# Two-bank product tiles in the first block, paired score matmuls, and groups 4,4,4,4,2,4 in one feed-forward stage

## The chip, the cores and the metric

The kernel runs on one core of one Trainium2 chip. The metric is the device time of one execution in microseconds (us). Three executions of the kernel before took 3538.49, 3545.83 and 3560.31 us; the median is 3545.83 us. The engines are named as the profile names them: PE (TensorE, matrix products; its weight loads are PEld), DVE (VectorE), ACT (ScalarE), POOL (GpSimd), SP (SyncE, which issues the DMAs). PSUM, the memory that PE writes its products to, has eight banks; one bank holds 512 float32 for each of the 128 partitions.

## The reference, cut to what matters

Two blocks follow each other on a sequence of 512 tokens of width 1024, all in float32. What the change touches is in the first block (two layers) and in the first feed-forward stage of the second block.

```python
# first block, for each of 2 layers
h = rms_norm(x, attn_norm[l]); proj = h @ w_in[l]
ret_o = retention(...)                  # 6 heads, chunks of 128
nsa_o = nsa(...)                        # 6 heads, 2 key/value groups; keys and values also compressed to 31 blocks
gm_o  = spatial_gating(...)
x = x + concat(ret_o, nsa_o, gm_o) @ w_out[l]
h = rms_norm(x, ffn_norm[l])
gate, up = split(h @ w_gate_up[l])      # 2 x 2816 columns
x = x + (silu(gate) * up) @ w_down[l]
# inside nsa, for a selected and a window branch
s = q @ k.T + bias; p = masked_softmax(s); o = p @ v
# second block, layer 0 (deltanet), its feed-forward, on 512 latent and 256 context columns
x = layernorm(alpha * x + g * ((silu(h @ w_gate) * (h @ w_up)) @ w_down))
# then layer 1: differential attention "da" and another feed-forward
```

## The kernel before, in words

Every float32 product of activations and weights is made of three matmuls (`mm3`, L216 to L220): both operands are split in a rounded part `hi` and a rest `lo`, and hi·hi, hi·lo and lo·hi are added in PSUM. A weight tile is loaded by a DMA on SP's queue (`wraw`, L205), `whi` is copied by ACT (L212), and `wlo` is made by DVE (L213).

Activations are held transposed, [128 features, tokens]. `gemm_b` makes a [128, 512] product in one PSUM bank (tile `gb`); `gemm_a` makes four token tiles t0 to t3 in four banks (tiles `ga0` to `ga3`) and calls an evacuation for each as soon as the last matmul of that tile is written down. In the first block's phase, `ps("g", ...)` gives one of four single banks (`g=4`, L856); the other four banks are s (2), o and c.

The program is written stage by stage, and a scheduler places each engine's instructions by priorities, taking its own estimates of when inputs are ready; afterwards each engine runs its list strictly in order. An instruction that must wait holds up all that stands behind it on its engine. Waits are semaphore counts of another engine's list. A wait is added wherever an instruction touches a tile that an instruction ahead of it in program order on another engine reads or writes, and tiles are what the tracking knows: two halves of one tile count as the same tile in the built program.

Places that the prediction speaks of:

- Feed-forward of the first block (`ffn1`): three groups of 8, 8 and 6 chunks. A chunk makes a gate product `pg` and an up product `pu` (24 matmuls each), and DVE and ACT turn them into an activation: `g` (L825), tanh (ACT, L826), `u` (L827), L828, L829, `ahi` (ACT, L830), `alo` (L831). After a group, eight down products, one for each m, are added to `x` by DVE (L836). Between them DVE also carries the filler `ada` (L901), a long product of its own.
- `gemm_a`: 14 of them in the two layers. The evacuations read the bank by ACT (L404, L410, L503, L695, L735), and by ACT and DVE for keys and values (`vt`, L493).
- Compression in `nsa`: for j = 0 and 1, a `gemm_b`, then `c` (DVE, L534), `X` (DVE, L538), and 64 small matmuls `pc` (L543) with `w1`, which a DMA brings (L531). In layer 0, DVE copies of bias tables (`biasc`) that come by DMA stand ahead of `c`.
- Scores in `nsa` (L614 to L625): for a pair of heads g = 0, 1 and a tile t, a matmul `S` (L619) on half of the partitions each, and DVE's bias and maximum (L622).
- The feed-forward `ffn2(0)` of the second block: the groups are FOURS (L31). After the last group, the down products of the context columns (256) and of the latent columns (512) are made for m = 0 to 7; DVE adds each to `xa` (L1459) and to two sums `lacc` (L1328, L1329); the layer norm's matmul `lns` (L1340) needs the finished sums. On PE `lns` of the latent columns stands ahead of the projections `da` of the next stage.

Of the kernel before, what the change touches and what calls it, by code (L numbers as in the profile page):

```python
# [14 lines left out]
F32 = mybir.dt.float32  # L15
# [7 lines left out]
P = 128  # L23
# [4 lines left out]
DFF = 2816  # L28
NFF = 22
GROUPS = ((0, 8), (8, 8), (16, 6))  # L30
FOURS = ((0, 4), (4, 4), (8, 4), (12, 4), (16, 4), (20, 2))  # L31
NEG = -1e30
NCMP = 31
NCTX = 256
# [155 lines left out]
class Kern:  # L190
# [29 lines left out]
        nc.tensor.matmul(out, l[1], r[0], start=False, stop=stop)  # L220

    def ps(self, tag, name):
        return self.psum.tile([P, 512], F32, name=name, tag=tag, bufs=self.banks[tag])

    def phase(self, **banks):

        self.banks = banks
        return self.tc.tile_pool(name="psum", bufs=1, space=PSUM, reuse_waits="tile")

    def gemm_a(self, h, dram, n, evac, tiles=NT):  # L230
# [221 lines left out]
    def nsa(self, l, mp, h, rt, rr, mix, early):  # L452
        tc, nc, a = self.tc, self.nc, self.a
        with tc.tile_pool(name=f"nsa{l}", bufs=1, reuse_waits="tile") as np_:
            kT = np_.tile([P, 2, T], F32, name="kT")
            vt = np_.tile([P, NT, 256], F32, name="vt")
            qT = np_.tile([P, 3, T], F32, name="qT")
# [6 lines left out]
            for g in range(2):  # L464
                s = slice(64 * g, 64 * g + 64)
# [7 lines left out]
            with tc.tile_pool(name=f"nsp{l}", bufs=1, reuse_waits="tile") as nw:  # L473
# [35 lines left out]
                for b in range(2):  # L509
                    ps = self.ps("s", "kps")  # L510
# [3 lines left out]
                for p in range(3):  # L514
                    ps = self.ps("s", "qps")
# [10 lines left out]
            with tc.tile_pool(name=f"cmp{l}", bufs=1, reuse_waits="tile") as cp, tc.tile_pool(name=f"nsw{l}", bufs=1, reuse_waits="tile") as nw:  # L526
                pc = self.ps("c", "pc")
                for j in range(2):
# [3 lines left out]
                    ps, = self.gemm_b(lambda k: (h[0][:, k], h[1][:, k]), KD, a["w_cmp"][l, j], ((0, T),))  # L532
                    c = cp.tile([P, T], F32, name="c", bufs=CB["c"])
# [6 lines left out]
                    for li in range(32):  # L540
                        for g in range(2):
                            s = slice(64 * g, 64 * g + 64)
# [10 lines left out]
                for g in range(2):  # L553
                    s = slice(64 * g, 64 * g + 64)
# [53 lines left out]
                for p in range(3):  # L608
                    po = self.ps("o", "po")
                    heads = (p, p + 3)  # L610
                    for b in range(2):
                        Z = nw.tile([P, 2, NT], F32, name="Z", bufs=2)
                        Pt = [[nw.tile([P, (t + 1) * P], F32, name=f"P{g}{t}", bufs=2) for t in range(NT)] for g in range(2)]
                        for t in range(NT):  # L614
                            n = (t + 1) * P
                            for g in range(2):
                                s = slice(64 * g, 64 * g + 64)
                                ps = self.ps("g", "S")
                                nc.tensor.matmul(ps[:, :n], qT[s, p, t * P:(t + 1) * P], kT[s, b, :n], start=True, stop=True)  # L619
                                sb = nw.tile([P, T], F32, name="sb", bufs=3)  # L620
                                mx = nw.tile([P, 1], F32, name="mx", bufs=4)
                                nc.vector.tensor_tensor_reduce(sb[:, :n], ps[:, :n], self.bias[:, heads[g], (3 - t) * P:],  # L622
                                                               -1.0, 3e38, op0=OP.add, op1=OP.min, accum_out=mx)
                                nc.scalar.activation(Pt[g][t], sb[:, :n], AF.Exp, bias=mx[:, 0:1], scale=-1.0,
                                                     accum_out=Z[:, g, t:t + 1])  # L625
                        early(3 + 2 * p + b, cp)
                        r = nw.tile([P, 2, NT], F32, name="r", bufs=2)
                        nc.vector.reciprocal(r, Z)
                        for g in range(2):
                            nc.vector.tensor_tensor(r[:, g], r[:, g], gate[:, :, heads[g] * 3 + 1 + b], op=OP.mult)  # L630
                        for t in range(NT):
                            for g in range(2):
                                nc.vector.tensor_scalar(Pt[g][t], Pt[g][t], r[:, g, t:t + 1], None, op0=OP.mult)
                        for j in range(NT):
                            n = (NT - j) * P
                            pts = []
                            for g in range(2):
                                ps = self.ps("s", "PT")
                                for t in range(j, NT):
                                    self.tpose(ps[:, (t - j) * P:(t - j + 1) * P], Pt[g][t][:, j * P:(j + 1) * P])  # L640
                                pt = nw.tile([P, T], F32, name="pt", bufs=3)
                                self.copy(pt[:, :n], ps[:, :n])
                                pts.append(pt)
                            for g in range(2):
                                nc.tensor.matmul(po[64 * g:64 * g + 64, j * P:], vt[:, j, b * P + 64 * g:b * P + 64 * g + 64],
                                                 pts[g][:, :n], start=b == 0 and j == 0, stop=False)
                    for g in range(2):
                        ps = self.ps("c", "PcT")
                        for t in range(NT):
                            self.tpose(ps[:NCMP, t * P:(t + 1) * P], scs[p][:, g, t])  # L650
                        pt = nw.tile([NCMP, T], F32, name="pct", bufs=2)
                        self.copy(pt, ps[:NCMP])
                        nc.tensor.matmul(po[64 * g:64 * g + 64], vc[:, 64 * g:64 * g + 64], pt, start=False, stop=True)
                    nc.scalar.activation(mix[0][:, p], po, AF.Copy)
                    nc.vector.tensor_tensor(mix[1][:, p], po, mix[0][:, p], op=OP.subtract)
# [188 lines left out]
    def first_block(self, depth=2):  # L844
        tc, nc = self.tc, self.nc
        self.xd = self.dram.tile([P, KD, T], F32, name="xd")
        self.xsrc = self.a["xT"]
        with tc.tile_pool(name="stat1", bufs=1, reuse_waits="tile") as self.stat, tc.tile_pool(name="mixc", bufs=1, reuse_waits="tile") as self.mixc:
            self.attn_norm = self.const("attn_norm", self.mixc)
            self.x_open()  # L850
            self.ffn_norm = self.const("ffn_norm", self.mixc)
            for nm in ("rope_c", "rope_s", "decay", "zeta", "xi", "cdec", "upper"):
                setattr(self, nm, self.const(nm, self.mixc))
            self.filler = self.ada()
            self.turns = TURNS[0]
            with self.phase(g=4, s=2, o=1, c=1) as self.psum:  # L856
                self.bias = self.mixc.tile([P, 6, T], F32, name="bias")
                self.biasc = self.mixc.tile([P, 6, NT, NCMP], F32, name="biasc")
                for l in range(depth):
                    self.layer1(l)  # L860
                    self.ffn1(l, l == depth - 1)
                    self.xsrc = self.xd
                for _ in self.filler:
                    pass
                self.filler = iter(())
            self.x_close()
# [996 lines left out]
```

## Time and profile before

| What | Value |
| --- | --- |
| Median of three runs | 3545.83 us (3538.49 to 3560.31) |
| Profiled execution | 3552.48 us, span 3550.7 us |
| Mean granted PE clock | 0.965 |
| PE busy | 3369.4 us, 95% of the span |
| PEld busy | 2814.8 us, 79% |
| DVE busy | 2343.1 us, 66% |
| ACT busy | 1504.6 us, 42% |
| POOL busy | 169.8 us, 5% |

All times in the rows further down are microseconds from the start of the span. In a timeline row the columns are: start, duration, engine, line, operation, output tile<-input tiles, shape, number of instructions, and in brackets the idle time of the engine just before it with what ended it. Matmuls overlap, so the distance from one start to the next is what a matmul costs, not its duration. The granted clock is a fraction of full speed: 1.00 is 2.4 GHz and 0.50 is 1.2 GHz.

### The profile page before, as it was taken

What the parts mean: (1) busy time and instruction counts of PE and PEld (TensorE: products, weight loads), DVE (VectorE), ACT (ScalarE), POOL (GpSimd) and SP (SyncE); (2) the same over time, 40 slices, a digit from 0 to 9 for tenths busy, and PEclk for the clock granted to TensorE, in tenths of its full rate; (3) what the DMA queues carried; (4) which work ended last, traced back from release to release, by engine and by line L of the source; (5) the groups of instructions that cost most, each with busy time, mean ns of one, the idle gap of its engine ahead of it and who ended that gap; (6) DMA issues with size and microseconds to landing.
All of it is one profiled execution on the core that took longest, in us unless ns stands there. A gap on an engine that the chain in (4) does not pass through costs nothing.

```text
span 3550.7 us, 54927 instructions
## 1 busy us (share of the span) xinstructions
PE 3369.4 (95%) x21774; PEld 2814.8 (79%) x21774; DVE 2343.1 (66%) x4749; ACT 1504.6 (42%) x2818; POOL 169.8 (5%) x161
## 2 busy tenths in 40 slices
PE   8999999989999999998999899999996999989998
PEld 6767888877678888777888777999996877778887
DVE  4556996545569854587778779676667566674336
ACT  4442322334433222456667657333336444452224
POOL 1000000010000000000010000111100000000000
PEclk9999999999999999999999899999998999999999
DMA  5212674331136843321111123222213211233333
GB/s 188 58 46 93 194 223 130 105 104 45 45 98 193 258 136 105 117 60 39 39 53 42 62 84 107 71 72 69 69 55 107 81 42 42 60 113 116 96 96 112
DMA packets 123306, 339.34 MB, mean 96 GB/s; under 512 B 17249, under 2 KB 35953, under 8 KB 122536
## 3 DMA queue, kind: packets, MB, share of 16 engines
q1 hardware_dynamic: 123048, 335.82, 30.9%
q8 instruction: 171, 2.80, 0.3%
q14 instruction: 87, 0.71, 0.1%
HBM read 324.16 MB, written 14.75 MB: 95 GB/s over the span
## 4 chain that ended last, share of the span: by engine, by line
PE 76%; DVE 11%; ACT 5%; issue 3%; DMA 3%; POOL 2%; SPq 0%; POOLq 0%; DVEq 0%; ACTq 0%
PE gb L218 14%; PE gb L219 14%; PE gb L220 14%; PE w L220 2%; PE w L218 2%; PE w L219 2%; DVE wlo L213 2%; DMA wada<-ada_w 2%; PE S L1595 2%; PE ga L220 2%; PE ga L218 2%; PE ga L219 2%; PE S L619 1%; PE da L220 1%; ACT whi L212 1%
## 5 line engine op out<-in xcount | busy, mean ns | idle before, releaser
L212 ACT ACTIVATE whi<-wraw 128x1024 fp32r<-128x1024 f32 (+4 forms) x519 | 472.5, 912 | 1081.7 <-PE gb L219 717.7
L213 DVE TENSOR_TENSOR wlo<-wraw,whi 128x1024 fp32r<-128x1024 f32 (+4 forms) x519 | 538.9, 1039 | 275.8 <-ACT whi L212 270.0
L220 PE MATMUL gb<-fhhi,wlo 128*128 128x512 f32 x704 | 276.1, 392 | 3.5 <-DVE wlo L213 3.4
L218 PE MATMUL gb<-fhhi,whi 128*128 128x512 f32 x704 | 275.7, 392 | 3.2 <-ACT fhhi L325 3.2
L219 PE MATMUL gb<-fhlo,whi 128*128 128x512 f32 x704 | 275.6, 392 | 0.0
L901 DVE CUSTOM_DVE_ANT_0 ada_t<-wada,ada_s 128x1024 f32<-128x1024 f32 x160 | 195.4, 1221 | 22.7 <-DMA wada<-ada_w 21.5
L218 PE MATMUL gb<-dhhi,whi 128*128 128x256 f32 (+1 forms) x528 | 193.8, 371 | 8.2 <-ACT dhhi L917 7.1
L218 PE MATMUL gb<-bhi,whi 128*128 128x512 f32 (+1 forms) x576 | 196.6, 343 | 2.6 <-ACT bhi L1816 1.8
L219 PE MATMUL gb<-blo,whi 128*128 128x256 f32 (+1 forms) x576 | 196.4, 342 | 0.1
L220 PE MATMUL gb<-bhi,wlo 128*128 128x512 f32 (+1 forms) x576 | 196.3, 342 | 0.1
L219 PE MATMUL gb<-dhlo,whi 128*128 128x256 f32 (+1 forms) x528 | 192.0, 365 | 0.1
L220 PE MATMUL gb<-dhhi,wlo 128*128 128x256 f32 (+1 forms) x528 | 190.5, 362 | 0.0
L218 PE MATMUL ga<-whi,hhi 128*128 128x384 f32 (+2 forms) x448 | 164.2, 366 | 14.8 <-ACT hhi L325 11.0
L219 PE MATMUL ga<-wlo,hhi 128*128 128x384 f32 (+2 forms) x448 | 163.3, 364 | 3.3 <-DVE wlo L213 3.3
L220 PE MATMUL ga<-whi,hlo 128*128 128x384 f32 (+2 forms) x448 | 163.2, 365 | 0.0
L220 PEld LDWEIGHTS gb<-fhhi,wlo 128*128 128x128 f32 x704 | 133.1, 189 | 33.9 <-DVE wlo L213 6.3
L1459 DVE SCALAR_TENSOR_TENSOR xa<-gb,mod,xa 128x256 f32<-128x256 f32 (+1 forms) x128 | 77.9, 615 | 123.0 <-PE gb L220 122.1
L218 PEld LDWEIGHTS gb<-fhhi,whi 128*128 128x128 f32 x704 | 133.0, 189 | 31.3 <-ACT fhhi L325 4.0
L219 PEld LDWEIGHTS gb<-fhlo,whi 128*128 128x128 f32 x704 | 133.2, 189 | 27.7
L219 PE MATMUL da<-wlo,ahhi 128*128 128x256 f32 x512 | 147.8, 289 | 1.0 <-DVE wlo L213 1.0
L218 PE MATMUL da<-whi,ahhi 128*128 128x256 f32 x512 | 148.0, 289 | 0.0
L220 PE MATMUL da<-whi,ahlo 128*128 128x256 f32 x512 | 147.1, 287 | 0.0
(569 smaller groups left out, 8749.8 us busy)
## 6 DMA issues: line engine op xcount, KB each, us to landing
wada<-ada_w SPq DMA_DIRECT2D x96, 512.0 KB, 4.4
wraw<-f_gate SPq DMA_DIRECT2D x52, 512.0 KB, 3.6
wraw<-f_up SPq DMA_DIRECT2D x52, 512.0 KB, 3.6
wraw<-w_gate SPq DMA_DIRECT2D x44, 512.0 KB, 4.2
wraw<-w_up SPq DMA_DIRECT2D x44, 512.0 KB, 4.0
wraw<-da_in SPq DMA_DIRECT2D x40, 512.0 KB, 3.6
wraw<-w_down SPq DMA_DIRECT2D x32, 512.0 KB, 3.8
wraw<-dn_in SPq DMA_DIRECT2D x32, 512.0 KB, 3.7
```

The source lines that it names most:

```text
L212: self.nc.scalar.activation(hi[:, :n], raw, AF.Copy)
L213: self.nc.vector.tensor_tensor(lo[:, :n], raw, hi[:, :n], op=OP.subtract)
L218: nc.tensor.matmul(out, l[0], r[0], start=start, stop=False)
L219: nc.tensor.matmul(out, l[0], r[1], start=False, stop=False)
L220: nc.tensor.matmul(out, l[1], r[0], start=False, stop=stop)
L619: nc.tensor.matmul(ps[:, :n], qT[s, p, t * P:(t + 1) * P], kT[s, b, :n], start=True, stop=True)
L901: nc.vector.tensor_tensor_reduce(th, w, s[:, st], 0.5, 0.0, op0=OP.mult, op1=OP.add, accum_out=self.mod[:, l, st, f:f + 1])
L1459: nc.vector.scalar_tensor_tensor(xs, p[:, :w], self.mod[:, l, st, 40 + m:41 + m], xs, op0=OP.mult, op1=OP.add)
L1595: nc.tensor.matmul(ps[:, k0:k0 + kn], qT[s, i, t * P:(t + 1) * P], kx, start=True, stop=True)
```

## The change

The first block's phase takes two tiles of two banks (`gg=2`) in place of four single banks. `ps("g", ...)` hands out the first half of such a tile, then, at the next call, its second half. The scores of a pair take one such tile, both matmuls are written down ahead of both evictions. FOURS, which is used in `ffn2(0)` alone, changes its last two groups from 4 and 2 chunks to 2 and 4.

```diff
-FOURS = ((0, 4), (4, 4), (8, 4), (12, 4), (16, 4), (20, 2))
+FOURS = ((0, 4), (4, 4), (8, 4), (12, 4), (16, 2), (18, 4))
...
     def ps(self, tag, name):
+        if tag == "g" and "gg" in self.banks:
+
+            if not self.half:
+                two = self.ps2(name)
+                self.half = [two[:, 512:]]
+                return two[:, :512]
+            return self.half.pop()
         return self.psum.tile([P, 512], F32, name=name, tag=tag, bufs=self.banks[tag])
+    def ps2(self, name):
+        self.half = []
+        return self.psum.tile([P, 1024], F32, name=name, tag="gg", bufs=self.banks["gg"])
...
-        self.banks = banks
+        self.banks, self.half = banks, []
...
                         for t in range(NT):
                             n = (t + 1) * P
+                            both = self.ps2("S")
                             for g in range(2):
                                 s = slice(64 * g, 64 * g + 64)
-                                ps = self.ps("g", "S")
-                                nc.tensor.matmul(ps[:, :n], qT[s, p, t * P:(t + 1) * P], kT[s, b, :n], start=True, stop=True)
+                                nc.tensor.matmul(both[:, 512 * g:512 * g + n], qT[s, p, t * P:(t + 1) * P], kT[s, b, :n], start=True, stop=True)
+                            for g in range(2):
+                                ps = both[:, 512 * g:512 * g + 512]
...
-            with self.phase(g=4, s=2, o=1, c=1) as self.psum:
+            with self.phase(gg=2, s=2, o=1, c=1) as self.psum:
```

The lists of the engines hold the same instructions, but their places and waits move. In the rows below, numbers behind a name tell buffers apart, and the brackets name the engines whose counts are waited for. In the changed kernel's rows L554, L841 to L849 are the lines L543, L828 to L836 of before (L838 and L840 are L825 and L827).

First place: PE, second group of layer 0's feed-forward, where the down product of m = 0 ends and that of m = 1 begins. Before:

```order
L218 MATMUL gb0_4745<-ahi_4726,whi_4742 128x512 [waits Activation_49]
L219 MATMUL gb0_4745<-alo_4727,whi_4742 128x512 [waits DVE_49]
L220 MATMUL gb0_4745<-ahi_4726,wlo_4741 128x512
L218 MATMUL gb0_4781<-ahi_4180,whi_4778 128x512
L219 MATMUL gb0_4781<-alo_4181,whi_4778 128x512
L220 MATMUL gb0_4781<-ahi_4180,wlo_4777 128x512
```

Now:

```order
L218 MATMUL gb0_4674<-ahi_4655,whi_4671 128x512 [waits Activation_49]
L219 MATMUL gb0_4674<-alo_4656,whi_4671 128x512 [waits DVE_49]
L220 MATMUL gb0_4674<-ahi_4655,wlo_4670 128x512
L218 MATMUL gb0_4674<-ahi_4116,whi_4707 128x512 [waits DVE_49]
L219 MATMUL gb0_4674<-alo_4117,whi_4707 128x512
L220 MATMUL gb0_4674<-ahi_4116,wlo_4706 128x512
```

The two products had tiles of their own and now share `gb0_4674`. The first matmul of m = 1 has a new wait; the DVE count it waits for is that of the addition L849 `x<-x,gb0_4674` of m = 0.

Second place: DVE, the last chunk of the same group, from its gate and up products to the first additions. Before:

```order
L825 TENSOR_TENSOR g_4723<-gb0_4667,rr_3170 128x512 [waits PE_49]
L213 TENSOR_TENSOR wlo_4741<-wraw_4739,whi_4742 128x1024 [waits DMAHW6_49,Activation_49]
L828 SCALAR_TENSOR_TENSOR g_4723<-th_4724,g_4723 128x512 [waits Activation_49]
L827 SCALAR_TENSOR_TENSOR u_4725<-gb0_4698,rr_3170 128x512 [waits PE_49]
L829 TENSOR_TENSOR u_4725<-u_4725,g_4723 128x512 [waits DVE_49]
L213 TENSOR_TENSOR wlo_4777<-wraw_4775,whi_4778 128x1024 [waits DMAHW7_49,Activation_49]
L831 TENSOR_TENSOR alo_4727<-u_4725,ahi_4726 128x512 [waits Activation_49]
```

Now:

```order
L213 TENSOR_TENSOR wlo_4670<-wraw_4668,whi_4671 128x1024 [waits DMAHW6_49,PE_49,Activation_49]
L838 TENSOR_TENSOR g_4652<-gb0_4597,rr_3119 128x512 [waits PE_49]
L840 SCALAR_TENSOR_TENSOR u_4654<-gb0_4597,rr_3119 128x512
L213 TENSOR_TENSOR wlo_4706<-wraw_4704,whi_4707 128x1024 [waits DMAHW7_49,Activation_49]
L841 SCALAR_TENSOR_TENSOR g_4652<-th_4653,g_4652 128x512 [waits Activation_49]
L842 TENSOR_TENSOR u_4654<-u_4654,g_4652 128x512 [waits DVE_49]
L844 TENSOR_TENSOR alo_4656<-u_4654,ahi_4655 128x512 [waits Activation_49]
```

The gate's `g` was made while PE worked on the up product. Now both products are one tile, `g` and `u` stand behind each other, and the PE count that L838 waits for is that of the up product's last matmul.

Third place: PE, layer 0's compression, the passage from the product of j = 0 (`gb0_674` before, first half of `gb0_670` now) to that of j = 1. Before:

```order
L220 MATMUL gb0_674<-hhi_119,wlo_670 128x512
L218 MATMUL gb0_776<-hhi_119,whi_773 128x512
L219 MATMUL gb0_776<-hlo_120,whi_773 128x512
L220 MATMUL gb0_776<-hhi_119,wlo_772 128x512
L218 MATMUL gb0_776<-hhi_119,whi_773 128x512
```

Now (the four rows `ga0` at the start are the last of 12 that stand between the two products):

```order
L220 MATMUL ga0_971<-whi_976,hlo_120 128x384
L218 MATMUL ga0_971<-whi_976,hhi_119 128x384
L219 MATMUL ga0_971<-wlo_975,hhi_119 128x384
L220 MATMUL ga0_971<-whi_976,hlo_120 128x384
L218 MATMUL gb0_670<-hhi_119,whi_769 128x512 [waits DVE_49]
L219 MATMUL gb0_670<-hlo_120,whi_769 128x512
L220 MATMUL gb0_670<-hhi_119,wlo_768 128x512
...
L218 MATMUL gb0_670<-hhi_119,whi_769 128x512
L219 MATMUL gb0_670<-hlo_120,whi_769 128x512
L554 MATMUL pc_660<-X_697,w1_661 64x31 [waits DMAHW0_49,DVE_49]
L220 MATMUL gb0_670<-hhi_119,wlo_768 128x512
```

The DVE count that the first matmul of j = 1 waits for is that of `c` of j = 0 (L534 before, L545 now). One `pc` matmul, which waits for `X` and for the DMA of `w1`, stands after 11 matmuls of j = 1; the other matmuls of the product stand behind it.

## Rows read from the trace of the kernel before

**Rows 1.** The page: busy time of PE and DVE; the chain that ended last, by engine.

```profile
PE 3369.4 (95%) x21774; PEld 2814.8 (79%) x21774; DVE 2343.1 (66%) x4749; ACT 1504.6 (42%) x2818; POOL 169.8 (5%) x161
PE 76%; DVE 11%; ACT 5%; issue 3%; DMA 3%; POOL 2%; SPq 0%; POOLq 0%; DVEq 0%; ACTq 0%
```

**Rows 2.** Timeline, second group's down products: m = 0 ends, m = 1 begins.

```profile
583.92 0.39 PE L220 MATMUL gb<-ahi,wlo 128*128 128x512 f32 x1
...
584.15 0.39 PE L218 MATMUL gb<-ahi,whi 128*128 128x512 f32 x1
...
584.35 0.69 DVE L836 TENSOR_TENSOR x<-x,gb 128x512 f32<-128x512 f32 x1 [2.29 <-PE gb L220]
```

**Rows 3.** Windows: busy us of PE, PEld, DVE, ACT, POOL; then PE clock, DMA.

```profile
475.00:500.00 25.00, 25.00 (x112) 20.70 (x111) 23.02 (x37) 5.14 (x5) 0.00 (x0) 1.00 0.72 226
...
585.00:610.00 25.00, 25.00 (x112) 20.68 (x112) 8.92 (x10) 4.48 (x5) 0.00 (x0) 1.00 0.33 92
```

**Rows 4.** Timeline, first group: last matmul of a down product, DVE's filler, its addition.

```profile
485.51 0.39 PE L220 MATMUL gb<-ahi,wlo 128*128 128x512 f32 x1
...
486.00 1.22 DVE L901 CUSTOM_DVE_ANT_0 ada_t<-wada,ada_s 128x1024 f32<-128x1024 f32 x1
...
488.41 0.68 DVE L836 TENSOR_TENSOR x<-x,gb 128x512 f32<-128x512 f32 x1
```

**Rows 5.** Timeline, third group's last chunk, from the up product's end.

```profile
687.71 0.69 DVE L827 SCALAR_TENSOR_TENSOR u<-gb,rr 128x512 f32<-128x512 f32 x1 [3.18 <-PE gb L220]
688.41 0.96 DVE L213 TENSOR_TENSOR wlo<-wraw,whi 128x768 fp32r<-128x768 f32 x1
...
690.01 0.63 ACT L830 ACTIVATE ahi<-u 128x512 fp32r<-128x512 f32 x1 [1.63 <-DVE u L829]
690.67 0.69 DVE L831 TENSOR_TENSOR alo<-u,ahi 128x512 fp32r<-128x512 f32 x1 [0.70 <-ACT ahi L830]
```

**Rows 6.** Timeline, a gemm_a: last matmul of t0, its successor, its evacuation.

```profile
53.78 0.35 PE L220 MATMUL ga<-whi,hlo 128*128 128x402 f32 x1
53.96 0.34 PE L218 MATMUL ga<-whi,hhi 128*128 128x402 f32 x1
...
54.16 0.60 ACT L503 ACTIVATE qx<-ga,rt 128x402 f32<-128x402 f32 x1
```

**Rows 7.** Timeline, layer 0's compression.

```profile
72.93 0.39 PE L220 MATMUL gb<-hhi,wlo 128*128 128x512 f32 x1
...
83.86 1.27 DVE L534 TENSOR_TENSOR c<-gb,rr 128x512 f32<-128x512 f32 x2
...
84.59 0.44 PE L218 MATMUL ga<-whi,hhi 128*128 128x384 f32 x1 [1.64 <-DVE c L534]
...
85.06 3.70 DVE L538 TENSOR_TENSOR X<-c,pe 128x992 f32<-128x992 f32 x2
...
89.46 0.21 PE L543 MATMUL pc<-X,w 64*64 64x31 f32 x1 [0.41 <-DMA w<-cmp_w]
```

**Rows 8.** Windows of the first block with PE waits, columns as in rows 3.

```profile
61.00:66.00 5.00, 2.22 (x11) 1.33 (x11) 2.93 (x8) 0.00 (x0) 2.88 (x2) 0.97 0.44 152
66.00:71.00 5.00, 4.12 (x13) 3.17 (x13) 1.25 (x2) 1.09 (x2) 2.44 (x4) 0.50 0.61 204
...
86.00:92.00 6.00, 5.59 (x33) 5.26 (x32) 4.58 (x4) 1.70 (x2) 0.00 (x0) 1.00 0.86 216
```

**Rows 9.** Waits of PE, 2640 to 2760: total, times, longest.

```profile
PE lns L1340 <- DVE lacc L1328: 18.0, 1, 18.0
```

**Rows 10.** Windows of the tail of ffn2(0), columns as in rows 3.

```profile
2600.00:2625.00 25.00, 25.00 (x144) 21.85 (x143) 13.39 (x20) 4.86 (x7) 2.83 (x2) 1.00 0.31 98
...
2680.66:2698.68 18.02, 0.00 (x0) 0.03 (x1) 18.02 (x36) 10.70 (x21) 0.00 (x0) 0.58 0.24 80
```

**Rows 11.** Timeline of PE: matmuls of 512 and of 256 columns.

```profile
2600.50 0.39 PE L220 MATMUL gb<-bhi,wlo 128*128 128x512 f32 x1
2600.73 0.28 PE L218 MATMUL gb<-bhi,whi 128*128 128x256 f32 x1
2600.85 0.28 PE L219 MATMUL gb<-blo,whi 128*128 128x256 f32 x1
```

**Rows 12.** DVE's groups by shape, 2640 to 2705: busy us, mean ns.

```profile
L213 DVE TENSOR_TENSOR wlo<-wraw,whi 128x256 fp32r<-128x256 f32 x16 | 6.6, 419 | 0.9 <-ACT whi L212 0.9
...
L1802 DVE TENSOR_TENSOR a22lo<-wraw,a22hi 128x512 fp32r<-128x512 f32 x1 | 0.7, 685 | 0.0
```

**Rows 13.** Timeline of PE, scores of 256 columns: a pair, later a single one.

```profile
165.27 0.70 PE L619 MATMUL S<-kT,qT 64*128 64x256 f32 x4
165.90 0.67 PE L645 MATMUL po<-pt,vt 128*64 128x256 f32 x4
...
177.32 0.70 PE L619 MATMUL S<-kT,qT 64*128 64x256 f32 x2
177.94 0.44 PE L645 MATMUL po<-pt,vt 128*64 128x128 f32 x4
```

## Prediction

> **What bounds the kernel now.** I read the page first: PE is busy for 95% of the span and makes 76% of the chain that ended last [rows 1]. So what PE waits for is paid in full almost everywhere, and what other engines do is paid only where PE waits for them. Then the waits and windows of the stages that the change touches. In the first block's feed-forward PE has 25.00 of 25 us [rows 3]: DVE is almost full there while it carries the filler (23.02 of 25) and nearly idle later (8.92). At the tail of ffn2(0) there is the one long wait, 18.0 us for `lacc` [rows 9], in which DVE works all the time (18.02 of 18.02) and PE not at all [rows 10]. Last, timelines of single places.
>
> The sum is made against the profiled execution (3552.5 us), which lies 6.7 us above the median of the runs; the result is then moved to the median.
>
> **A. Down products of the first block.** Before, a down product is followed by the next one 0.23 us after its last matmul, and DVE's addition runs beside it: it starts 0.43 us after that matmul and ends at 1.12 us [rows 2]. Now m = 1, 3, 5, 7 share a tile with m = 0, 2, 4, 6, and their first matmul waits for that addition. A PE that waited for DVE went on 0.1 us after DVE's end: the first of two `c` ends near 84.49, PE starts at 84.59 [rows 7]. So the next matmul comes at 1.22 instead of 0.23: 0.99 us a wait, less 0.23 for each matmul of other tiles that the list has in between. There are 4 x 3 groups x 2 layers = 24 such waits. Group 2: none in between, 8 x 0.99 = 7.9. Group 3: one in between at six, none at two: 6 x 0.76 + 2 x 0.99 = 6.5. Group 1 has two in between at most places, at least 4.2 us for its 8; but there DVE is late, since fillers of 1.22 us stand ahead of the addition, which starts 2.90 us after the matmul in place of 0.43 [rows 4]. That would be up to 3.0 us a wait. A PE that waits lets DVE catch up, and between two additions DVE has some 5.8 us of work (one `wlo`, three fillers) against PE's 24 x 0.23 = 5.4; I take 1.5 us a wait, 12.
>
> The Trainium skill, Perfetto Trace Analysis, section Optimizing Tensor Performance (Matmuls), says that independent matmul groups should rotate through different PSUM banks, so that the evacuation of one overlaps the next one's matmuls. The trace of before agrees [rows 2]; the halves are still different banks, so by this rule A would be 0. I take the wait that stands in the list, not the bank.
>
> **B. The last chunk of each group.** `g` could be made while PE was at the up product; now DVE's read of the first half waits for the end of the second. Before, the chain from the up product's last matmul (0.43 us ahead of L827, so 687.28) to the end of `alo` (691.36) takes 4.08 us [rows 5]. To it come the `g` that stood earlier (0.69) and L828 (0.69). With one `wlo` in between, as listed, `alo` ends near 5.5 in group 3 and 5.8 in group 2. PE wants it 16 matmuls after the up product in group 3 (3.9 us) and 22 after in group 2 (5.2): with 0.1 us of release 1.8 and 0.7 us, of which 0.2 was paid before. In group 1 two fillers stand in that chain, 2.6 us. Together (1.6 + 0.7 + 2.6) x 2 layers = 10. Bounds 4 (no filler or `wlo` in the way) and 16.
>
> **C. `gemm_a`.** Here t1 waits for the evacuation of t0, and t3 for that of t2. The evacuation ends 0.98 us after the last matmul [rows 6], 1.08 with the release, against a step of 0.18; four matmuls in between leave 0.2 us. For t3, ACT has t1's evacuation ahead of t2's (0.58 more), which leaves about 0.8. With 14 of them 14 us at most places alike; some have transposes in between, so 12. Bounds 2 and 25 (28 x 0.9, nothing in between).
>
> **D. Compression.** In layer 0, PE ended the first product at 73.2 [rows 7], and would end the 12 `ga` matmuls at 75.3. It now waits for `c`, which stands behind DVE's copies of tables that arrive by DMA: 84.6. That is 9.3 us, less some 2 us that C has already made PE late. After 11 matmuls (2.5 us) `pc` waits for `w1`, which was there at 89.46: 2.4 more. The 1.64 and 0.41 us of waits of before go [rows 7]: +7.6, in layer 1, without tables, 1.4: 9. Bounds 4 and 13.
>
> **E. Clock.** In 61 to 66 PE was busy 2.22 of 5 us, and in the next 5 us the clock was granted at 0.50; after the wait of 1.64 us it stayed 1.00 [rows 8]. The wait of D is of the first kind: 5 us at half speed, +2.5. Those of A to C are of the second: 0. Bounds 0 and 25 (rival 2).
>
> **F. Groups 2 and 4.** The last group's matmuls run inside the stretch that DVE bounds; the group ahead of it runs where PE has 25.00 of 25 [rows 10]. A chunk's down products are 8 x 3 matmuls of 256 and 512 columns at 0.12 and 0.23 us [rows 11], 8.4 us; two chunks move, so PE saves 16.8 us ahead of the tail and fills its wait there. But the tail's 16 `wlo` go from 256 columns (0.42 us) to 512 (0.69) [rows 12]: DVE's stretch, and with it `lns`, ends 4.3 us later. -12.5. Bounds -17 (the longer `wlo` hidden) and -6 (late weights queue another 6.7 us). The same work is late next: `lns`, still behind `lacc`, with some 6 us less to wait.
>
> **G. Scores.** A pair that stands together costs what one does: 0.63 for four instructions, 0.62 for two [rows 13]. But the lists place 25 of 48 pairs together now, 27 before: 0. Bounds -16 (all together) and +5.
>
> **Sum.** A 7.9 + 6.5 + 12 = 26.4; with B 10, C 12, D 9, E 2.5, F -12.5, G 0: **+47**. 3552.5 + 47 = 3600 for an execution like the profiled one, 3545.8 + 47 = **3593** at the median. Changes of under 1% (35 us) are about what a measurement of this kernel can tell from none.
>
> **Rivals.**
>
> 1. The new waits cost little: the scheduler's matmuls in between and a DVE that PE's pauses have relieved cover most. For it: group 1 and `gemm_a` have two to five matmuls in between. Against it: groups 2 and 3 have none or one, and 1.12 us is a fixed chain [rows 2]. At the low bounds A is 19, B 4, C 2, D 4, E 0; with F +16, so 3562. Were banks alone to decide, A, C and D's wait would be 0 and the sum near 0: 3546. Chance 0.2 for all of this. The page named in A stands behind its last step.
>
> 2. The clock falls. If each of the ten longest pauses of group 1 (B's two, A's eight) is followed by 5 us at half speed, as after 66 us [rows 8], 25 us come on top: 3618. Against it: the pause of 1.64 us with its clock of 1.00 [rows 8]. Chance 0.1. The Trainium skill, TensorE: Matmul & The Clock Gate, section on PSUM-queue depth-cycling, tells of a kernel whose clock swung because PE paused briefly between matmul groups. Its pauses are the kind that A makes; the trace here shows none yet.
>
> 3. Faster: evacuations end before PE comes back to the tile, so only F and G act. The place is the first matmul of each second half; it decides at 0.23 us (the next matmul's natural start) plus what stands in between, against 1.22. Then -12.5 gives 3533, and with all pairs of scores together, which the lists don't show, 3517. Chance 0.04, half of it beyond 1%.
>
> 4. F gains little: DVE bounds both groups ahead and the tail. Against it: DVE had 13.39 of 25 us at 2600 [rows 10]. It would add 6 us to the forecast, 3599, inside its range.
>
> That the change does not do what it says is G: it pairs scores in the program, the lists don't follow.
>
> **Numbers.** The forecast (with rival 4) has 0.66, rival 1 0.2, rival 2 0.1, rival 3 0.04. Its own range is 3572 to 3612: A +-8, B +-6, C +-10, D +-4, F +-6, taken as independent, with some us for the runs' spread. To leave out 2 in 10 the range reaches down to rival 1's 3560 and up to 3615. Slower by over 1% (above 3581): most of the forecast, rival 2: 0.70. Within 1%: rival 1, the forecast's low end, half of rival 3: 0.28. Faster: 0.02.
>
> **What would show it.** A: PE waits `gb` <- DVE L849, 24 times, 0.7 to 2 us; none means rival 1 or 3. B: waits for `ahi` or `alo` at group ends. C: `ga` <- ACT, 0.2 and 0.8 us. D: a wait of 7 us for `c` near 77 and one for `w1`, then a clock of 0.50. F: `lns` <- `lacc` near 12 us in place of 18.0. G: as many pairs of `S` as before. The forecast is wrong if the waits are there but short, or if the clock in the feed-forward falls below 1.00.

## The result, and the profile after

| What | Before | After |
| --- | --- | --- |
| Median, four runs each | 3543.47 us (3538.49 to 3560.31) | 3587.14 us (3582.89 to 3590.22) |
| Ratio | | 1.0109, interval 1.0086 to 1.0132 |
| Profiled execution, its span | 3552.48, 3550.7 us | 3590.22, 3588.4 us |
| Mean granted PE clock | 0.965 | 0.966 |

The change makes the kernel slower, by 43.7 us at the medians and by 37.7 us between the two profiled executions (before's lies 9.0 us above its median, after's 3.1). The forecast was +47.

The page after, busy time and chain by engine; these lines answer to [rows 1]:

```profile
PE 3387.9 (94%) x21774; PEld 2810.8 (78%) x21774; DVE 2345.7 (65%) x4749; ACT 1503.2 (42%) x2818; POOL 170.3 (5%) x161
PE 75%; DVE 12%; ACT 5%; issue 4%; DMA 3%; POOL 1%; SPq 0%; POOLq 0%; ACTq 0%; DVEq 0%
```

No engine has more work: the instructions are the same. By these pages PE's idle time grows by 19.2 us (the span less the busy time: 181.3 before, 200.5 after) and its busy time by 18.5, so it both stands still longer and takes longer for the same matmuls. Where that happens is seen when the two traces are laid on each other by stage. The marks are PE's first gate matmul of a feed-forward, the last matmul of the up products of a group, and the last of its down products. Each step is how much later PE reaches a mark than before, less what it was late at the mark ahead:

| Stretch up to the mark | Layer 0 | Layer 1 |
| --- | --- | --- |
| mixer (scores, compression, `gemm_a`), up to the first gate matmul | +5.2 | -5.8 |
| group 1, gate and up | +2.4 | +2.1 |
| group 1, down | +11.0 | +16.1 |
| group 2, gate and up | -1.0 | -1.6 |
| group 2, down | +5.0 | +5.0 |
| group 3, gate and up | 0.0 | 0.0 |
| group 3, down | +5.8 | +7.4 |
| first block's feed-forwards, sum | +23.3 | +28.9 |

Behind the first block the deltanet stage, whose program is the same, is 6.1 us shorter, and the stretch with F (from the deltanet's layer norm to the first projection `da`; "the last stretch" in what follows) is 8.6 us shorter. Together 52.2 - 0.6 - 6.1 - 8.6 = 36.9 of the 37.7 us.

**The down products.** Timeline of the second group of layer 0 (without the weight loads): m = 0 ends, DVE adds it, m = 1 begins. It answers to [rows 2]:

```profile
602.06 0.40 PE L220 MATMUL gb<-ahi,wlo 128*128 128x512 f32 x1
...
602.49 0.69 DVE L849 TENSOR_TENSOR x<-x,gb 128x512 f32<-128x512 f32 x1 [0.82 <-PE gb L220]
...
603.23 0.50 PE L218 MATMUL gb<-ahi,whi 128*128 128x512 f32 x1 [0.78 <-DVE x L849]
...
603.57 0.40 PE L219 MATMUL gb<-alo,whi 128*128 128x512 f32 x1
```

The next matmul starts 1.17 us after the last one of m = 0, where it was 0.23, and 0.05 us after DVE's addition ends. The first matmul after the pause also takes 0.34 us to its successor, not 0.23. Such a pause comes four times in each group.

The other three places carry another name. PE's waits in the second group (total, times, longest):

```profile
PE gb L218 <- ACT whi L212: 2.6, 3, 0.9
PE gb L218 <- DVE x L849: 0.8, 1, 0.8
PE gb L219 <- DVE alo L844: 0.2, 1, 0.2
```

These three wait for the addition too. The place between m = 2 and m = 3, with PE's weight load (PEld):

```profile
614.21 1.06 ACT L212 ACTIVATE whi<-wraw 128x1024 fp32r<-128x1024 f32 x1 [4.33 <-PE gb L219]
614.44 0.69 DVE L849 TENSOR_TENSOR x<-x,gb 128x512 f32<-128x512 f32 x1 [3.30 <-PE gb L220]
615.24 0.19 PEld L218 LDWEIGHTS gb<-ahi,whi 128*128 128x128 f32 x1 [1.27 <-issue]
615.27 0.47 PE L218 MATMUL gb<-ahi,whi 128*128 128x512 f32 x1 [0.87 <-ACT whi L212]
```

The weight load starts 0.11 us after the addition's end (615.13), but 0.03 us ahead of the copy's (615.27). So it can't have waited for this `whi`, which belongs to a later product. The other two places are alike.

In groups 1 and 3 the name is right. There PE's list has the first matmuls of the product after next, which has another tile, between the two products that share one. At the end of group 1 the product after next is a gate product, so the names show it:

```profile
501.73 0.39 PE L220 MATMUL gb<-ahi,wlo 128*128 128x512 f32 x1
501.93 1.06 ACT L212 ACTIVATE whi<-wraw 128x1024 fp32r<-128x1024 f32 x1 [3.92 <-PE gb L219]
503.04 0.50 PE L218 MATMUL gb<-fhhi,whi 128*128 128x512 f32 x1 [0.92 <-ACT whi L212]
...
504.17 0.50 PE L218 MATMUL gb<-ahi,whi 128*128 128x512 f32 x1 [0.39 <-DVE x L849]
```

The matmul that was to fill the pause waits itself: the program has two buffers for `whi`, and the copy into the free one starts only when the product that has just ended has read it. Of the 24 places in the two layers PE waits for such a `whi` at 13 and for the addition itself at 11 (at 2 of the 13 for the addition as well, behind the matmuls in between). Both begin at the end of the product ahead and cost about the same, so over a whole feed-forward one counts the waits by the place, not by the name.

**Group 1** has more: PE, DVE, ACT busy in 5 us stretches of layer 0, with PE's granted clock behind POOL's column. They answer to [rows 3], where PE had 25.00 of 25 us at 1.00:

```profile
455.00:460.00 5.00, 4.69 (x21) 3.57 (x19) 5.00 (x9) 1.49 (x2) 0.00 (x0) 1.00 0.73 220
460.00:465.00 5.00, 2.64 (x6) 1.65 (x7) 5.00 (x9) 1.69 (x2) 0.00 (x0) 0.80 0.57 158
465.00:470.00 5.00, 5.00 (x13) 3.86 (x12) 4.65 (x8) 0.00 (x0) 0.00 (x0) 0.52 0.79 224
470.00:475.00 5.00, 5.00 (x23) 4.11 (x22) 2.02 (x3) 1.06 (x1) 0.00 (x0) 1.00 0.47 153
```

PE idles 2.4 of the 5 us from 460, and in the next 5 us the clock is granted at 0.52, close to the lower level (1.2 GHz): 13 matmuls instead of 23. In the loss of speed alone that is 5 x (0.20 + 0.48) = 3.4 us, an upper bound for its cost, since the sum also counts stretches in which PE stands idle; in layer 1 the same sum over 1190 to 1240 is 3.4 too. The pauses ahead of it, from PE's timeline:

```profile
460.82 0.51 PE L218 MATMUL gb<-ahi,whi 128*128 128x512 f32 x1 [1.13 <-ACT ahi L843]
461.91 0.50 PE L219 MATMUL gb<-alo,whi 128*128 128x512 f32 x1 [0.58 <-DVE alo L844]
463.60 0.79 PE L218 MATMUL gb<-ahi,whi 128*128 128x512 f32 x1 [0.96 <-ACT whi L212]
```

The first two are the last chunk's chain (`u` to `ahi` to `alo`), the third is the first matmul of m = 2, set ahead of m = 1, waiting for its `whi`. In layer 1 one more shows what DVE's list does to such a wait:

```profile
1232.23 1.22 DVE L914 CUSTOM_DVE_ANT_0 ada_t<-wada,ada_s 128x1024 f32<-128x1024 f32 x1 [0.77 <-DMA wada<-ada_w]
...
1233.38 0.68 DVE L849 TENSOR_TENSOR x<-x,gb 128x512 f32<-128x512 f32 x1
...
1234.12 0.56 PE L218 MATMUL gb<-ahi,whi 128*128 128x512 f32 x1 [2.86 <-DVE x L849]
```

The addition stands behind a filler that itself waited 0.77 us for a DMA, so PE pays the filler's input: 2.86 us.

**The mixers.** PE's waits from 60 to 360 us; the first and the third answer to [rows 7]:

```profile
PE gb L218 <- DVE c L545: 7.9, 1, 7.9
PE qps L461 <- DVE qn L495: 2.9, 3, 1.5
...
PE pc L554 <- DMA w<-cmp_w: 0.7, 1, 0.7
...
PE ga L218 <- ACT zz L706: 0.3, 1, 0.3
PE ga L218 <- ACT rx L746: 0.3, 1, 0.3
```

The wait for `c` is there (7.3 forecast), the one for `w1` is 0.7 and not 2.4. Before, `ga` waited 1.6 us for `c`, and `qps` 4.5 us. The clock after the wait, 5 us stretches:

```profile
73.00:78.00 5.00, 0.28 (x2) 0.00 (x0) 0.89 (x3) 0.94 (x5) 1.28 (x2) 0.93 0.91 329
78.00:83.00 5.00, 1.80 (x4) 1.49 (x5) 3.30 (x5) 0.94 (x5) 1.28 (x3) 0.50 0.38 101
```

`gemm_a` shows almost no wait. The place of [rows 6] now, from its timeline:

```profile
53.80 0.34 PE L220 MATMUL ga<-whi,hlo 128*128 128x402 f32 x1
...
54.18 0.60 ACT L514 ACTIVATE qx<-ga,rt 128x402 f32<-128x402 f32 x1
54.34 0.35 PE L220 MATMUL ga<-whi,hlo 128*128 128x402 f32 x1
54.53 0.75 PE L218 MATMUL ga<-whi,hhi 128*128 128x402 f32 x2
...
55.12 0.34 PE L219 MATMUL ga<-wlo,hhi 128*128 128x402 f32 x1
```

Two matmuls take 0.59 us from start to start where two steps of 0.18 were due: 0.2 us, and nothing further at t3.

**The tail of ffn2(0).** The wait of [rows 9], and DVE's group of [rows 12], 2670 to 2735:

```profile
PE lns L1353 <- DVE lacc L1341: 8.8, 1, 8.8
```

```profile
L213 DVE TENSOR_TENSOR wlo<-wraw,whi 128x512 fp32r<-128x512 f32 x16 | 10.9, 684 | 2.0 <-ACT whi L212 1.9
```

PE waits 9.2 us less. DVE's tail, from the first addition of context columns to the last `lacc`, grows from 40.0 to 46.7 us.

### The profile page after: what moved, and what is told of

The parts are those of the page before. It is cut to its first block, busy times and chain, and to the rows that moved or that the text cites. A ratio compares the mean times of both kernels' runs of the same rounds, so it can differ in the third digit from the quotient of the medians.

```text
span 3588.4 us, 54932 instructions
## 1 busy us (share of the span) xinstructions
PE 3387.9 (94%) x21774; PEld 2810.8 (78%) x21774; DVE 2345.7 (65%) x4749; ACT 1503.2 (42%) x2818; POOL 170.3 (5%) x161
## 4 chain that ended last, share of the span: by engine, by line
PE 75%; DVE 12%; ACT 5%; issue 4%; DMA 3%; POOL 1%; SPq 0%; POOLq 0%; ACTq 0%; DVEq 0%
PE gb L218 14%; PE gb L219 13%; PE gb L220 13%; DVE wlo L213 3%; PE w L220 2%; PE w L219 2%; PE w L218 2%; ACT whi L212 2%; PE S L1608 2%; PE ga L218 2%; PE ga L219 2%; PE ga L220 2%; DMA wada<-ada_w 2%; PE da L220 1%; PE da L219 1%
## 5 line engine op out<-in xcount | busy, mean ns | idle before, releaser
L218 PE MATMUL gb<-bhi,whi 128*128 128x256 f32 (+1 forms) x576 | 195.2, 341 | 2.4 <-ACT whi L212 1.6
L220 PE MATMUL gb<-bhi,wlo 128*128 128x256 f32 (+1 forms) x576 | 195.4, 341 | 0.3 <-DVE wlo L213 0.2
L218 PE MATMUL ga<-whi,hhi 128*128 128x384 f32 (+2 forms) x448 | 164.0, 369 | 13.8 <-ACT hhi L336 10.9
L218 PE MATMUL gb<-ahi,whi 128*128 128x512 f32 x352 | 142.4, 407 | 26.2 <-ACT whi L212 16.1
```

The lines of the kernel that those rows point to most:

```text
L218: nc.tensor.matmul(out, l[0], r[0], start=start, stop=False)
```

## Experiments

The theory: nearly all of the loss is the tile, not the bank. Two products that share a tile wait for each other's evacuation, at the first block's down products (A) and gate and up products (B). Rivals: the loss is the mixers' (C, D), or the clock alone, or F. Ratios are against the kernel before, run on the same chip.

**e1, FOURS alone.**

```diff
-FOURS = ((0, 4), (4, 4), (8, 4), (12, 4), (16, 4), (20, 2))
+FOURS = ((0, 4), (4, 4), (8, 4), (12, 4), (16, 2), (18, 4))
```

> Only the groups 4,4,4,4,2,4; the first block as before. Theory (the shared tiles cost, the groups gain): the profile of the change shows the stage of the tail 8.6 us shorter, so 9 us less than before, about 3535 us, with the wait of the layer norm for its sums near 12 us instead of 18.0. Rival (the groups gain nothing, the 8.6 us are the run's clock): as before, about 3543 us.

3536.7 us, 0.9969 (0.9949 to 0.999): 0.3% faster. The last stretch is 7.8 us shorter in its profile, and `lns` waits 8.8 us, as in the whole change. F is a gain, and of the size of its low half; the wait was expected near 12 us.

**e2, all but FOURS** (the change with the old FOURS line).

> The change with the old groups 4,4,4,4,4,2. Theory: the first block's two-bank tiles cost 52 us alone, so about 3595 us. Rival (the groups gain nothing): as the change, about 3587 us.

3605.0 us, 1.0165 (1.0144 to 1.0186). The feed-forwards lose what they lose in the whole change (down products +10.7, +5.0, +5.9 and +14.0, +5.1, +5.7 us), the last stretch is 0.35 us shorter. So the loss is the first block's; at 3605 us it is some 10 us above what was expected.

**e3, the first feed-forwards alternate over two tiles.** Two tiles are taken at once; successive products get the first half of one, the first half of the other, then the second halves. Products next to each other then never share a tile; the banks and their number stay.

```diff
         if tag == "g" and "gg" in self.banks:
             if not self.half:
                 two = self.ps2(name)
+                if self.inter:
+                    one = self.ps2(name)
+                    self.half = [two[:, 512:], one[:, 512:], two[:, :512]]
+                    return one[:, :512]
...
+            self.half, self.inter = [], True      # at the start of ffn1, False at its end
```

> The change, but in the first block's feed-forward the halves are handed out in another order: first halves of both tiles, then both second halves, so that no product shares a tile with the one just ahead of it. Theory (A and B: waits of a product for the reader of the half just ahead, and reads that wait for the second half): the 45 us that the feed-forwards of the two layers are longer go, about 3542 us, with no wait of 0.7 us or more of a down product for the addition. Rival (the mixers' stretches C and D carry the loss): stays above 3575 us.

3552.65 us, 1.0017 (1.0003 to 1.0031). Steps of the two feed-forwards: +0.3 and +0.9 us in place of +23.3 and +28.9. This settles the cause of the loss there: same banks, same two-bank tiles, only the order in which halves are handed out. The scheduler's lists follow from that order, and most of the matmuls that groups 1 and 3 had in between are gone from them too; whether a third buffer for `whi` and `wlo` would have saved those 13 waits with tiles shared was not run. The time misses the expected 3542 by 10.6 us. That lies in the mixers, whose program is the change's: they are 8.2 and 1.8 us longer than before, the change's +5.2 and -5.8, and in them e3's profile lost 39.3 us of speed to clocks below 1.00, the change's 29.0.

**e5 and e6, one half of that each.** In e5 only the down products alternate, in e6 only gate and up products (`self.half, self.inter = [], True` ahead of the down loop or of the chunk loop alone).

> The change with alternate halves for the feed-forward's down products alone: takes A away (a product waits for the addition of the one just ahead), leaves B (gate and up share a tile). From the stage times, A is the part from the last u of a group to its last addition, B the rest. Theory (A is most): of the 51 us that both cost, 35 to 40 go, about 3550 us, and the last chunk's waits for ahi and alo stay. Rival (B is most, since the late activations also delay the first down product): 15 to 20 us go, 3570 us.

> The change with alternate halves for gate and up alone: takes B away, leaves A. Theory: 10 to 15 us go, about 3574 us, and 24 waits of 0.7 us or more stay at the down products. Rival (B is most): 30 us or more go, 3557 us.

e5: 3547.17 us, 1.0000 (0.9985 to 1.0015); e6: 3585.74 us, 1.01 (1.0079 to 1.0122). With e5, which leaves B, the feed-forwards lose 1.6 and 2.6 us, 4.2 in all. With e6, which leaves A, the down products lose 7.9, 4.5, 4.5 and 13.4, 4.5, 4.4 us. A is what costs; B alone nearly nothing. For e6 some 3574 us were expected. By the marks 15.2 us do go (52.2 to 37.0), but in its profile other stretches, whose program is the same, are 11.3 us longer than in the change's, and the medians of the two aren't told apart (1.01 and 1.0109).

e6 also tells the clock's share. Its layer 0 where the whole change fell to 0.52:

```profile
460.00:465.00 5.00, 2.82 (x10) 1.81 (x11) 5.00 (x8) 1.63 (x2) 0.00 (x0) 1.00 0.74 208
465.00:470.00 5.00, 5.00 (x24) 4.12 (x23) 4.80 (x9) 0.51 (x1) 0.00 (x0) 1.00 0.77 243
```

Nearly the same pauses (0.82, 0.58 and 0.97 us), no fall, and group 1's down products 3.1 us cheaper. From the second of these pauses to the next pause behind them the change takes 16.7 us (461.91 to 478.63) and e6 13.8 (461.72 to 475.53): of the 3.4 us of lost speed 2.9 are paid. In layer 1 the clock of e6 did fall, to 0.67 and 0.50, 5.1 us of lost speed. So almost the same pauses were followed by a fall in one kernel and by none in the other.

**e4, `gemm_a` alternates too** (e3 and the same two lines around `gemm_a`).

> As the run before, and also in gemm_a the four token tiles take the halves in alternation, so t2's last matmuls wait for the reader of t0 with t1's matmuls in between. By the prediction's term C another 12 us go: about 3530 us. By the stage times of the two profiles (the mixers are only some 4 us longer in sum): at most 4 us go, 3538 to 3542 us.

3564.98 us, 1.0045 (1.0029 to 1.0061), no faster than e3: the mixers are 10.2 us and 4.9 us longer than before, as against 8.2 and 1.8 with e3; most of its 12 us over e3 lies behind the first block, in the stages from `da` on, 8.0 us, whose program is the same. Nothing was lost in `gemm_a` that alternation could give back; C falls.

**e8, the compression's products get tiles of their own** (e3 and `self.half = []` ahead of each `w_cmp` product and of `gemm_a`).

> The feed-forward with alternate halves (3553 us), and the two compression products in tiles of their own, so that the second does not wait for c of the first. Term D as predicted (9 us lost there): 3544 us. Rival (the wait of 7.9 us only takes the place of later waits of the same stretch; between the first score and the last score the change wins 8.6 us back): within 3 us, 3550 to 3556 us; the wait for c goes in both.

3542.69 us, 0.9988 (0.9971 to 1.0004), 0.3% under e3 by the ratios, some 10 us. PE goes on to `gemm_a` and waits there:

```profile
PE ga L218 <- DVE c L551: 6.6, 1, 6.6
```

So most of the wait only moves. Its profile is 15.7 us ahead of e3's at the first gate matmul, but up to that mark e3 lost 20.5 us of speed to clocks below 1.00 and e8 5.1: the half speed at 120 to 135 that before, the change, e1, e3 and e5 show is missing. In layer 1 its mixer is 8.0 us shorter than e3's and lost 8.6 us less (18.8 and 10.2). Cleared of that, 0.3 us are left in layer 0 and nothing in layer 1, so the 3544 expected came true by the clock and not by D. It isn't one lucky execution: the mean granted clock of e8's twelve runs is 0.9678, of e3's 0.9657, and of the kernel before on these two chips 0.9651 and 0.9653; 0.0021 of the time is some 7 us. Why this program runs at a higher clock stays open, and e3 and e8 come from different chips, with intervals (+-0.0014 and +-0.0017) near their difference.

**e7, all pairs of scores together** (e3, and each `S` matmul placed with high priority, so all 48 pairs stand together, not 25).

> The feed-forward with alternate halves (3553 us), and the two score matmuls of a pair at high priority, so that all 48 pairs of the two layers stand together in PE's list, 25 before. If PE bounds that stretch, 23 more pairs save 0.42 to 1.05 us each, about 16 us: 3537 us. Rival (waits for the softmax and the copies bound it): within 5 us, 3548 to 3556 us.

3552.01 us, 1.0006 (0.9991 to 1.002): nothing against e3. PE's groups of `S` and `po` (the two longest shapes) up to 361 us, first of the whole change, then of e7:

```profile
L630 PE MATMUL S<-kT,qT 64*128 64x512 f32 x24 | 11.1, 724 | 0.0
L630 PE MATMUL S<-kT,qT 64*128 64x384 f32 x24 | 10.2, 599 | 0.0
L658 PE MATMUL po<-pt,vt 128*64 128x512 f32 x24 | 8.9, 618 | 0.0
...
L658 PE MATMUL po<-pt,vt 128*64 128x384 f32 x24 | 6.5, 512 | 0.1
```

```profile
L663 PE MATMUL po<-pt,vt 128*64 128x384 f32 x24 | 9.6, 512 | 0.9 <-ACT pt L297 0.8
L663 PE MATMUL po<-pt,vt 128*64 128x512 f32 x24 | 8.7, 618 | 0.7 <-DVE pt L299 0.7
L635 PE MATMUL S<-kT,qT 64*128 64x512 f32 x24 | 8.1, 699 | 0.2 <-DVE mx L640 0.2
L635 PE MATMUL S<-kT,qT 64*128 64x384 f32 x24 | 6.9, 590 | 0.0
```

Over all shapes of this view `S` goes from 33.1 to 22.6 us (before: 31.4) and `po`, with the compressed branch, from 26.2 to 32.5 (before: 24.0). The `po` products of two heads fill half of the columns each, and where two stand side by side they cost what one does: from 167.01 the next start comes 1.0 us after four instructions of 512 columns, and it comes 1.0 us after two alone as well (at three places of e7; the two at 150.00 last 1.07). In PE's lists for both layers, of 108 `po` products 60 follow another directly before, 53 in the change, 39 in e7. So one pairing was paid with the other for the larger part; the 4.2 us that are left in this view don't show in the median.

The places of those two, from PE's timeline of e7:

```profile
150.00 1.07 PE L663 MATMUL po<-pt,vt 128*64 128x512 f32 x2
...
167.01 1.08 PE L663 MATMUL po<-pt,vt 128*64 128x512 f32 x4 [0.71 <-DVE pt L299]
168.02 0.77 PE L465 MATMUL PT<-c_ident,P 128*128 128x128 f32 x5
```

**e9, filler later.** The theory's guess for group 1: DVE's fillers ahead of the addition lengthen the waits. The filler steps between down products go from one each to 0, 1, 2 in groups 1, 2, 3.

```diff
-                    next(self.filler, None)
+                    for _ in range((0, 1, 2)[gi]):
+                        next(self.filler, None)
```

> The change, with DVE's filler moved from the first group's down products to the third group's (two steps a product there instead of one). In the change the first group's down products take 55.0 and 59.9 us in the two layers, 44.0 before, the third's 38.7 and 40.2, 32.8 before. Theory (A is dear where DVE is full: PE's pause puts off DVE's additions, and with them the weight splits behind them): without filler the first group's take about 50 us as the second group's do (48.5), and the third's, now with filler, grow by 4 us or more. Rival (the late weights, brought by DMAs that compete, make the difference): the first group's stay at 54 us or more in both layers.

3595.7 us, 1.0138 (1.0115 to 1.016). It doesn't test the guess, since the fillers didn't move: DVE still carries 25 and 20 of them in group 1's down products of the two layers and none in group 3's, as in the change (before: 22, 17 and none), and the down products of group 1 cost as much (+10.9, +15.9). What the fillers cost as a whole stays open; a single wait of 2.86 us behind one is seen at 1234.12.

**e10, groups 4, 4, 4, 4, 1, 5** (kernel before and that line).

> The first block as before, groups 4,4,4,4,1,5 in ffn2(0): one more chunk moved out of the PE-bound stretch. Theory (F as measured: PE saves 8.4 us a chunk ahead of the tail, DVE's tail grows by some 3.4 us a chunk): the wait of the layer norm falls from 8.8 to 3 to 4 us and the stage is 4 to 5 us shorter than with 2 and 4, about 3532 us. Rival (five activation tiles in five buffers hold up the first blocks of the last group, or the tail of DVE grows as fast as PE saves): 3536 us or more.

3538.29 us, 0.9975 (0.9959 to 0.9992). `lns` waits less again:

```profile
PE lns L1340 <- DVE lacc L1328: 3.7, 1, 3.7
```

Its last stretch is 10.8 us shorter, e1's 7.8. The wait came as expected (3 to 4 us), the expected 3532 us didn't: 3538 falls to the rival, and the times of e1 and e10 aren't told apart. e1 has the lowest ratio of all: 0.3% under the kernel before and 1.4% under the change.

## Why the prediction was right, and where its terms were off

The direction, the size and the main cause were right: 3587 against 3593, and A is the largest term. That the sum came so close is luck, since large errors cancel: the feed-forwards lose 15.8 us more than A and B together (52.2 for 36.4), the mixers 24.1 less than C, D and E (-0.6 for 23.5), F gains 3.9 less, and 6.1 come back in the deltanet stage, whose program is the same.

- **A, 26.4 forecast.** e6, less 5.1 us of lost clock, gives 39.3 - 5.1 = 34.2 us, all in excess of the forecast: group 1 16.2 (12), group 2 9.1 (7.9), group 3 8.9 (6.5). As the 5.1 count idle stretches too, A lies between 34.2 and 39.3. In group 2 a wait costs 1.13 us, not 0.99: the pause also slows the first matmul behind it (0.34 for 0.23), and three of four first matmuls start 1.26 us after the last of the product ahead, not 1.18. In group 3 the matmul of another tile in between was to hide 0.23 us of each; it hid nothing, because it waits itself for its `whi`, 0.75 us. The step that failed is "less 0.23 for each matmul of other tiles that the list has in between". In group 1 the matmuls in between wait in the same way (0.92 at 503.04), and DVE's list makes single waits behind them nearly as long as the bound of 3.0 (2.86 at 1234.12).
- **B, 10 forecast.** Alone 4.2 us (e5), the lower bound. The waits for `ahi` and `alo` at group ends are there in the whole change, 1.7 us in the first group of layer 0, but in e6, without B, they are there too (0.82, 0.58). They belong to A and B together: of the 52.2 us, 34.2 are A's, 4.2 B's, at most 6.8 the clock's, and the last 7 or more appear only with both.
- **The rule on banks** (the Trainium skill, Perfetto Trace Analysis, Optimizing Tensor Performance (Matmuls)) would have made A 0. The halves are different banks and PE waits at all 24 places; e3 has the same banks and doesn't wait there. Here the tile is the unit that decides.
- **C, 12 forecast; refuted.** Waits of 0.2 to 0.3 us at three or four places, and e4 gains nothing. The failed step is the 0.8 us for t3 "at most places alike": the first place has 0.2 for both tiles together.
- **D and E, 9 and 2.5 forecast.** The wait for `c` came (7.9), `w1` is 0.7 instead of 2.4. The half speed behind it came too (0.50 at 78 to 83), but in place of the one that the kernel before has at 66 to 71 [rows 8]: up to the first gate matmul both profiles lose 18.8 us of speed, so E adds nothing. In all, the mixers came out at -0.6 in place of C, D and E's 23.5. Of these 24 us 10 are the profile of before, which lost 20.5 us of speed in layer 1's mixer, the one of after 10.2. e1 runs the same first block as before; against its profile the mixers of the change are +7.1 and +1.9 us. Cleared of lost speed, each up to the kernel's own first gate matmul (17.1 us in e1 against 18.8, 13.7 against 10.2), that is +5.4 and +5.4: 11 us for C and D together, forecast 21. In layer 0 it is the wait for `c`, 7.9, and `w1`, less what shrank (`ga` on `c` 1.6, `qps` 4.5 to 2.9), which the forecast counted for `ga` alone. What layer 1's 5 us consist of stays open.
- **Rival 2, the clock in group 1,** was given 25 us and a chance of 0.1. It is real, at up to 6.8 us: the forecast's last sentence, that it is wrong if the clock in the feed-forward falls below 1.00, came true in part. The pause of 1.64 us that kept 1.00 [rows 8] was a single one; here pauses of 1.13, 0.58 and 0.96 us follow each other. The Trainium skill, TensorE: Matmul & The Clock Gate, section on PSUM-queue depth-cycling, tells of such swings from brief pauses; the trace after agrees (0.52), e6's layer 0 with like pauses doesn't (1.00).
- **F, -12.5 forecast.** -8.6 in the profile, -7.8 to -11.0 in those of the other kernels with this line. Two of its sizes are off: the tail begins 15.2 us earlier within the stage, not 16.8 (533.0 us behind the deltanet's layer norm before, 517.8 after), and DVE's tail grows by 6.7 us, not 4.3, since its idle places grow as well as its `wlo`: 15.2 - 6.7 = 8.5. That the wait would shrink "some 6 us" to 12 was an error of the text: what PE gains there it gains out of that wait, so -12.5 meant 5.5; it is 8.8.
- **G, 0 forecast.** The lists did leave the pairs as they were. But placing all of them together gains nothing either (e7), which the bound of -16 didn't see: `po` pairs in the same way and pays.

## What to carry to other kernels

Where waits are kept per tile, two independent products in one tile are one product: hand the halves out so that neighbours never share a tile (e3), before thinking of banks. Price such a wait as the full chain, last matmul to first matmul, plus the slow start behind it. Count a matmul that the list sets in between as help only if its own inputs are ready: here its weights had to wait for the same product. On an engine that stands behind a backlog, add the backlog, its DMA waits too. When a wait at the end of a stage has one engine idle and the other full, move work of the idle one into it, and count what the full one gets in return (e1, e10).

## What was not expected of the hardware

`po` matmuls of two heads, on different halves of the columns, run together as the score matmuls on different halves of the rows do: 1.0 us from start to start for a pair of 512 columns and for one. And the clock falls or stays after almost the same chain of pauses (0.52 in the whole change, 1.00 in e6, at the same place), worth 3 us in layer 0. The speed lost in layer 1's mixer differs by 10.3 us between two executions of one program there (20.5 before, 10.2 in e10), and e10's mixer is 10.3 us shorter. A few us in a mixer are no evidence until the clock is taken out, and the lost speed has to be summed up to the same mark of the program, not up to the same time.
